# Two arrays woven into one on one Trainium2 core: every 32 KiB row of the loads moved as two pieces of 16 KiB

## Chip, cores and metric

One core of a Trainium2 chip runs the kernel. The metric is the device time of one execution in microseconds (us); smaller is better. The kernel before took 314.11 us, the median of three runs (314.11, 314.11 and 314.13 us).

## What is computed

Two float32 arrays of 32 x 256 x 1024 elements are woven: the even places of the last axis of the result come from x, the odd places from y.

```python
result = np.zeros((batch, seq, dim * 2), dtype=np.float32)
result[..., 0::2] = x
result[..., 1::2] = y
```

Nothing is calculated. Each input is 33.55 MB, the result 67.11 MB, so 67.11 MB are read and 67.11 MB written.

## The kernel before, in words

The flat arrays are cut into n = 8 tiles. A tile of x (or y) is 128 partitions x 8192 float32, that is 128 rows of 32 KiB, 4 MiB in all. A tile of the result is twice that, and is worked in two halves (h = 0 and h = 1) of 4 MiB. On the chip there are two buffers for x tiles (`xt`), two for y tiles (`yt`), used by even and odd tiles, and two for result halves (`ot`), one for each h. DMA means a transfer between the chip's outer memory and these buffers.

Three engines take part, each with its own list in program order:

- **SyncE (SP) issues the loads**, on its own ring of DMA work (q1 in the profile). The first x tile comes as two DMAs of 2 MiB (L42, L43), whose rows are 16 KiB each, since they take half of the columns. Then for each tile k, L50 loads x and L53 loads y, 4 MiB each with rows of 32 KiB. From k = 2 on, L50 waits until the second x copy of tile k - 2 is done (`woven`, L48), and L53 until its second y copy is done (L52), because they overwrite the buffers that these copies read.
- **VectorE (DVE) weaves.** For each tile and half, L67 copies half of the x tile to the even columns of `ot[h]`, and L70 copies half of the y tile to the odd ones. Before L67 of half 0 it waits for the x load (L60); before L67 of either half for the store that last read `ot[h]` (L64); before L70 of half 0 for the y load (L69). Each copy raises `woven` by 1. The order is L67 and L70 of half 0, then L67 and L70 of half 1.
- **ScalarE (ACT) issues the stores**, on another ring (q10). For each tile and half it waits for `woven` (L74) and issues one DMA of 4 MiB with rows of 32 KiB (L83). The very first half is stored in two DMAs: a quarter of the columns (L77, 1 MiB, rows of 8 KiB) and the rest (L81, 3 MiB, rows of 24 KiB).

The two rings are served by the same 16 DMA engines. A DMA of 128 rows gives every engine 8 rows; the trace has one packet record for each row, and one small record of 4 bytes on each engine that signals the end.

In what follows, x3 is the load of tile 3 of x, y3 that of y, and S0_3 and S1_3 are the stores of the two halves of tile 3.

Of the kernel before, what the change touches and what calls it, by code (L numbers as in the profile page):

```python
# [3 lines left out]


def _interleave(nc, x, y, out):
    P = 128
    W = 8192
    H = W // 2  # L10

    total = 1
    for s in x.shape:
        total *= s
    n = total // (P * W)
    assert n * P * W == total

    def rows(ap, names, k):
        flat = ap.rearrange("b s d -> (b s d)")
        return flat[k * names : (k + 1) * names].rearrange("(p w) -> p w", p=P)  # L20

    fp32 = mybir.dt.float32
    xt = [nc.alloc_sbuf_tensor(f"xt{b}", [P, W], fp32).ap() for b in (0, 1)]
    yt = [nc.alloc_sbuf_tensor(f"yt{b}", [P, W], fp32).ap() for b in (0, 1)]
    ot = [nc.alloc_sbuf_tensor(f"ot{b}", [P, W], fp32).ap() for b in (0, 1)]

    xsem = [nc.alloc_semaphore(f"xsem{b}") for b in (0, 1)]
    hsem = nc.alloc_semaphore("hsem")
    qsem = nc.alloc_semaphore("qsem")
    ysem = [nc.alloc_semaphore(f"ysem{b}") for b in (0, 1)]  # L30
    woven = nc.alloc_semaphore("woven")
    osem = [nc.alloc_semaphore(f"osem{b}") for b in (0, 1)]


    cuts = [0, W // 4, W]
    parts = [slice(a, b) for a, b in zip(cuts, cuts[1:])]

    xs = [rows(x, P * W, k) for k in range(n)]
    ys = [rows(y, P * W, k) for k in range(n)]
    os_ = [rows(out, 2 * P * W, k) for k in range(n)]  # L40

    nc.sync.dma_start(out=xt[0][:, :H], in_=xs[0][:, :H]).then_inc(xsem[0], 16)  # L42
    nc.sync.dma_start(out=xt[0][:, H:], in_=xs[0][:, H:]).then_inc(hsem, 16)  # L43

    for k in range(n):
        b = k % 2
        if k >= 2:
            nc.sync.wait_ge(woven, 4 * (k - 2) + 3)  # L48
        if k:
            nc.sync.dma_start(out=xt[b], in_=xs[k]).then_inc(xsem[b], 16)  # L50
        if k >= 2:
            nc.sync.wait_ge(woven, 4 * (k - 2) + 4)  # L52
        nc.sync.dma_start(out=yt[b], in_=ys[k]).then_inc(ysem[b], 16)  # L53

    for k in range(n):
        b = k % 2
        for h in (0, 1):
            c = slice(h * H, (h + 1) * H)
            if h == 0:
                nc.vector.wait_ge(xsem[b], 16 * (k // 2 + 1))  # L60
            elif k == 0:
                nc.vector.wait_ge(hsem, 16)
            if k:
                nc.vector.wait_ge(osem[h], 16 * k)  # L64
            if (k, h) == (1, 0):
                nc.vector.wait_ge(qsem, 16)
            nc.vector.tensor_copy(out=ot[h][:, 0::2], in_=xt[b][:, c]).then_inc(woven, 1)  # L67
            if h == 0:
                nc.vector.wait_ge(ysem[b], 16 * (k // 2 + 1))  # L69
            nc.vector.tensor_copy(out=ot[h][:, 1::2], in_=yt[b][:, c]).then_inc(woven, 1)  # L70

    for k in range(n):
        for h in (0, 1):
            nc.scalar.wait_ge(woven, 4 * k + 2 * h + 2)  # L74
            if (k, h) == (0, 0):
                for c in parts[:-1]:
                    nc.scalar.dma_start(  # L77
                        out=os_[k][:, c], in_=ot[h][:, c]
                    ).then_inc(qsem, 16)
                c = parts[-1]  # L80
                nc.scalar.dma_start(out=os_[k][:, c], in_=ot[h][:, c]).then_inc(osem[h], 16)  # L81
                continue
            nc.scalar.dma_start(  # L83
                out=os_[k][:, h * W : (h + 1) * W], in_=ot[h]
            ).then_inc(osem[h], 16)

    nc.scalar.wait_ge(osem[0], 16 * n)
    used = sorted(s.num for s in [*xsem, hsem, qsem, *ysem, woven, osem[0]])
    assert used == list(range(used[0], used[-1] + 1)), used
    nc.scalar.sem_clear(range(used[0], used[-1] + 1))  # L90
    nc.sync.nop(nofuse=True).wait_op(osem[1], 16 * n, "sem-ge").then_inc(
        osem[1], -16 * n
    )


def kernel(tc, x, y, out):
    nc = tc.nc
    tc.close()
    tc.compile()

    _interleave(nc, x, y, out)

    blocks = nc.main_func.blocks
    for engine in (mybir.EngineType.SP, mybir.EngineType.SP):
        opening = blocks[0].instructions
        at, moved = next(
            (b, i)
            for b in blocks[1:]
            for i in b.instructions
            if i.engine == engine and i.opcode == "DMACopy"  # L110
        )
        assert not (moved.sync_info and moved.sync_info.on_wait)
        body = at.instructions
        body.remove(moved)
        gate = next(
            n
            for n, i in enumerate(opening)
            if i.engine == engine and i.opcode == "Drain"
        )
        opening.insert(gate, moved)  # L120
        at.instructions = body
        blocks[0].instructions = opening


# [1 line left out]
_INS = ['x', 'y']  # L126
_OUTS = [((32, 256, 2048), 'float32')]


# [23 lines left out]
```

## Time and profile before

| What | Value | Where from |
|---|---|---|
| median of three runs | 314.11 us | the times |
| span of the profiled execution, first to last instruction | 312.9 us | the page |
| the profiled execution's own time | 312.9 us of span, and about 1.2 us around it, taken from the median | worked out: 314.11 - 312.9 |
| bytes moved, mean rate | 134.22 MB, 429 GB/s | the page, part 2 |
| DMA packets | 4896, of which 544 end signals | the page, part 2 |
| VectorE busy | 72.0 us, 32 copies, 2.29 us each | the page, parts 1 and 5 |
| store of 4 MiB, issue to landing, median | 34.1 us | the page, part 6 |
| load of x (4 MiB), of y (4 MiB), issue to landing, median | 24.3 us, 41.5 us | the page, part 6 |

How to read it: the span is cut into 40 slices, and a digit tells in tenths how busy an engine (or the mean of the 16 DMA engines) was in a slice. The share of a ring is the time that its packets took, as a share of what 16 engines had in the span. "Issue to landing" runs from the instruction that hands a DMA to its ring until all its bytes have arrived, so it contains the time that the DMA stands behind others in its ring. A wait is put down to what ended it.

### The profile page before, as it was taken

How to read it: one execution, taken by the hardware profiler on the slowest of the kernel's cores; microseconds unless marked ns; L12 is line 12 of the kernel's file. 1: busy time of each engine (PE TensorE's matmuls, PEld its weight loads, DVE VectorE, ACT ScalarE, POOL GpSimd, SP SyncE). 2: the span in 40 equal slices, each digit the busy share in tenths (PEclk: the TensorE clock that was granted, in tenths of full speed). 3: DMA queues.
4: the chain of work that ended last, by engine and by line, in shares of the span. 5: the costliest groups of instructions: out<-in, count | busy, mean ns of one | idle time of the engine just before them, and what ended most of it. 6: DMA issues, size and time to landing. Idle time of an engine off the chain costs nothing.

```text
span 312.9 us, 114 instructions
## 1 busy us (share of the span) xinstructions
DVE 72.0 (23%) x32; POOL 0.2 (0%) x4
## 2 busy tenths in 40 slices
DVE  0216000501305023050220503205032050415410
POOL 0000000000000000000000000000000000000000
DMA  8999999999999999999999999999999999999998
GB/s 337 467 402 436 436 402 419 452 457 415 427 444 411 461 402 469 402 469 402 469 402 465 406 440 432 423 448 402 469 402 469 402 469 402 469 402 448 423 423 381
DMA packets 4896, 134.22 MB, mean 429 GB/s; under 512 B 544, under 2 KB 544, under 8 KB 544
## 3 DMA queue, kind: packets, MB, share of 16 engines
q1 hardware_dynamic: 2448, 67.11, 50.1%
q10 hardware_dynamic: 2448, 67.11, 49.7%
HBM read 67.11 MB, written 67.11 MB: 429 GB/s over the span
## 4 chain that ended last, share of the span: by engine, by line
DMA 82%; DVE 12%; issue 0%
DMA out_dram<-ot 76%; DMA yt<-in_y_dram 6%; DVE ot L70 6%; DVE ot L67 6%
## 5 line engine op out<-in xcount | busy, mean ns | idle before, releaser
L67 DVE COPY ot<-xt 128x4096 f32<-128x4096 f32 x16 | 36.7, 2295 | 213.8 <-DMA out_dram<-ot 206.5
L70 DVE COPY ot<-yt 128x4096 f32<-128x4096 f32 x16 | 36.6, 2288 | 12.3 <-DMA yt<-in_y_dram 12.3
L137 POOL MEMSET const-bfloat16-1.0<- 128x1 bf16 x1 | 0.1, 103 | 0.0
L137 POOL MEMSET const-uint8-127<- 128x1 uint8 x1 | 0.1, 102 | 0.0
L137 POOL MEMSET const-float32-0.0<- 128x1 f32 x1 | 0.1, 100 | 0.2 <-issue 0.2
L137 POOL MEMSET const-float32-1.0<- 128x1 f32 x1 | 0.1, 99 | 0.0
## 6 DMA issues: line engine op xcount, KB each, us to landing
out_dram<-ot ACTq DMA_DIRECT2D x15, 4096.0 KB, 34.1
yt<-in_y_dram SPq DMA_DIRECT2D x8, 4096.0 KB, 41.5
xt<-in_x_dram SPq DMA_DIRECT2D x7, 4096.0 KB, 24.3
xt<-in_x_dram SPq DMA_DIRECT2D x2, 2048.0 KB, 9.5
out_dram<-ot ACTq DMA_DIRECT2D x1, 3072.0 KB, 32.8
out_dram<-ot ACTq DMA_DIRECT2D x1, 1024.0 KB, 16.3
```

Of the source, the lines that this page charges most:

```text
L67: nc.vector.tensor_copy(out=ot[h][:, 0::2], in_=xt[b][:, c]).then_inc(woven, 1)
L70: nc.vector.tensor_copy(out=ot[h][:, 1::2], in_=yt[b][:, c]).then_inc(woven, 1)
L137: nc = _bacc.Bacc("TRN2", target_bir_lowering=False, num_devices=1)
```

## The change

The loads L50 and L53 no longer go through the usual call but through a helper that lays out both sides, the outer memory's and the buffer's, as 128 rows x 2 pieces x 16 KiB before it makes the DMA. The bytes, the buffers, the semaphores, the waits and the order of issue stay as they were. There are 15 such loads (7 of x, 8 of y). The two first loads of x (L42, L43) and all stores are unchanged.

```diff
+QUEUES = {
+    mybir.EngineType.SP: "qSPDynamicHW",
+    mybir.EngineType.Activation: "qActDynamicHW",
+}
+
+
+def _piece_copy(engine, out, in_, s):
+
+    ins, outs = (
+        engine.lower_ap_dma(ap.rearrange("p (s w) -> p s w", s=s)) for ap in (in_, out)
+    )
+    return engine.add_instruction(
+        mybir.InstDMACopy(
+            mode="Copy",
+            name=engine.bass.get_next_instruction_name(),
+            engine=engine.engine,
+            ins=ins,
+            outs=outs,
+            queue=QUEUES[engine.engine],
+        )
+    )
...
         if k:
-            nc.sync.dma_start(out=xt[b], in_=xs[k]).then_inc(xsem[b], 16)
+            _piece_copy(nc.sync, xt[b], xs[k], 2).then_inc(xsem[b], 16)
         if k >= 2:
             nc.sync.wait_ge(woven, 4 * (k - 2) + 4)
-        nc.sync.dma_start(out=yt[b], in_=ys[k]).then_inc(ysem[b], 16)
+        _piece_copy(nc.sync, yt[b], ys[k], 2).then_inc(ysem[b], 16)
```

## The prediction

> **What bounds the kernel now.** The chain of waits is read first, because it names a culprit; its opening and one later round:
>
> ```profile
> 1.90 19.99 DMA yt<-in_y_dram
> 21.89 0.02 issue
> 21.91 2.29 DVE ot L70
> 24.20 2.20 DVE ot L67
> 26.41 2.21 DVE ot L70
> 28.62 0.02 issue
> 28.64 48.16 DMA out_dram<-ot
> ...
> 120.08 34.17 DMA out_dram<-ot
> ```
>
> By this the stores bound the kernel: VectorE waits for a store, weaves for 4.5 us, and the next store takes 34.17 us. The waits say the same (L67 waited 206.5 us for stores, L70 once for a y load, 12.3 us). But 34.17 us for 4 MiB is long, so the second view is whether the DMA engines had anything better to do. The page's slices and rings:
>
> ```profile
> DMA  8999999999999999999999999999999999999998
> q1 hardware_dynamic: 2448, 67.11, 50.1%
> q10 hardware_dynamic: 2448, 67.11, 49.7%
> ```
>
> and busy time by stretches (columns: stretch, its length, VectorE and GpSimd busy, clock, DMA share, GB/s):
>
> ```profile
> 2.00:22.00 20.00, 2.39 (x2) 0.00 (x0) 1.00 1.01 433
> 57.00:250.00 193.00, 44.97 (x20) 0.00 (x0) 1.00 1.00 433
> ```
>
> 50.1% + 49.7% is 99.8% of 16 engines: the 16 DMA engines are never idle, from the first packet (0.99 us after the first issue, by the trace's packet records) to the last (0.38 us before the end of the span). Loads alone (2 to 22 us) run at 433 GB/s, and loads mixed with stores (57 to 250 us) at the same 433. So the bound is the sum of all packets. The chain only tells whose turn it was. The time can change in two ways: packets cost more or fewer ns per byte, or the engines fall idle somewhere.
>
> **How two rings share an engine.** This decides the second way, and the first store shows it. Its two DMAs have rows of 8 and 24 KiB and run beside loads with rows of 32 KiB. The DMA view of 29 to 40 us (8 KiB stores in q10):
>
> ```profile
> q1 hardware_dynamic: 136, 3.93, 85.3%
> q10 hardware_dynamic: 123, 0.92, 19.7%
> ```
>
> and of 42 to 56 us (24 KiB):
>
> ```profile
> q1 hardware_dynamic: 127, 3.64, 60.2%
> q10 hardware_dynamic: 112, 2.75, 45.6%
> ```
>
> The columns are packets, MB, share of time. The packet counts are nearly equal both times (136 to 123, 127 to 112), the bytes 4.3 to 1 and 1.3 to 1. The rings take turns packet by packet, whatever a packet holds. The prices in the packet records are 309, 611, 912 and 1213 ns for 8, 16, 24 and 32 KiB. Turns of 309 + 1213 ns, 8 a DMA, make 12.2 us; the store of 1 MiB landed 16.3 us after issue, of which 4.4 us were before its first packet.
>
> **The change part by part.**
>
> (a) *More packets.* 15 loads x 128 rows become two packets each: 1920 more, 120 for each engine. Upper price: 2 x 611 - 1213 = 9 ns, times 120 = 1.08 us. Lower price, from the end signals in the same records while loads ran alone: one engine's second half of x0 (8 packets of 16 KiB) took 4.862 us from signal to signal, y0 (8 of 32 KiB) 9.681; 2 x 4.862 - 9.681 = 0.043 us, less one signal of 0.009, is 0.034 us for a load of 4 MiB, and 15 loads make 0.51 us. I take 0.6, near the second, since it is time between events and not packets' own durations, which overlap a little (they sum to 311.84 us for each engine in 311.48 us of time). A gain is excluded: a 16 KiB packet costs more than half of a 32 KiB packet in both readings.
>
> (b) *Turns.* A turn of the two rings was 32 KiB against 32 KiB. It becomes 16 KiB of load against 32 KiB of store: while both have work, stores get two thirds. Call U the time of 4 MiB at full rate: two stores and two loads took 38.72 us (stores landed at 115.53 and 154.25), so U = 9.68. A store beside loads took 2 U = 19.4; it now takes 8 turns x (1.209 + 0.607) = 14.5 us, in which the loads advance by half a tile array.
>
> Before, the loads ran ahead: two tiles were loaded or in line when the first store began, and equal turns kept that lead; the stores held the weaving back. Now the lead melts. By hand: the first store packets come at 28 us, with x1 at 0.67. S0_0 takes 8 x (0.307 + 0.607) + 8 x (0.908 + 0.607) = 19.4 us, to 47.4; loads gain 1.0. S1_0 takes 14.5, to 61.9; y1 lands near 57. S0_1 and S1_1 run from about 62.5 to 91.5; x2 lands near 85, and y2 lacks 0.77 at 91.5. The store ring is empty, and y2 has all turns until 99. From tile 2 on, VectorE waits at L70 for y.
>
> Steady state, counted from y_k's last packet: 0.36 us to landing (x0: last signal at 6.97, L67 at 7.33), 0.02, L70 for 2.29, 0.04 until ACT issues S0_k (24.20 to 24.24): 2.71 us. Its first packet comes 0.99 us later on idle rings (L42), 4.4 us later behind queued loads (L77: 24.24 to 28.64). S0_k and S1_k take 2 x 14.5. So S1_k ends 32.7 to 36.1 us after y_k, while y_(k+1) ends after 2 U of loads and 2 U of stores, at 38.7. When y lands, the store ring has been dry for 2.6 to 6 us. In mid-run this costs nothing: x_(k+1) and y_(k+1) stand in the load ring, since their buffers came free when tile k - 1 was woven. The L67 copies, the other L70 and SP's issues (0.33 us) lie beside it.
>
> (c) *The end.* After y7 no load is left to cover that dry spell. Before, y7's last packet passed by 278 us, with 35 us of stores queued behind it. Now nothing moves from y7's last packet until S0_7's first: 2.71 + 0.99 = 3.70 us. The engines then also start cold: the first 16 KiB packets of L42 took 1145 ns and more where 611 is usual, and its 8 packets 0.8 to 1.1 us longer than the next 8. A cold store is not in the trace; 0 to 1.1 us, I take 0.4. S1_7 is woven (4.4 us) under S0_7 (9.7 us).
>
> Sum: 0.6 + 3.7 + 0.4 = **+4.7 us**, with bounds 0.51 + 3.7 + 0 = 4.2 and 1.08 + 3.7 + 1.1 = 5.9. The profiled span of 312.9 becomes 317.6; 1.2 us lie outside it. On the median: 314.11 + 4.7 = **318.8 us**, likeliest range 318.3 to 320.0.
>
> **Rivals.**
>
> *Equal turns stay.* If the two pieces of a row, contiguous on both sides, go in one turn, the loads keep their lead, the end stays covered, and only (a) remains: 314.6 to 315.2. For it: no transfer before has two pieces in a row. Against: each row's packet in the two windows ended the turn. Chance 0.09. The Trainium skill, DMA: Bandwidth & Descriptors, section Queues, rings and completion order, speaks for this rival: an engine is said to drain a whole packet of typically 9 to 17 descriptors from one ring before it switches. By that rule two pieces of a row would share a turn, and the time would be this rival's. The trace disagrees where it can be seen: the counts 136 to 123 are turns of one row each, and an engine's 8 rows of the 1 MiB store, drained at once, would have taken 8 x 0.309 = 2.5 us and not 12.
>
> *Partial cover.* If stores get less than two thirds, S1_6 is still moving when y7 lands and hides part of the 3.7 us. The point is 38.7 us for 2 stores that begin 3.7 to 7.1 us after y: 31.6 to 35 us instead of 29, so a share of 0.55 to 0.61. Time 315.2 to 318.3. Chance 0.08.
>
> *Not slower: the pieces are joined again.* Somewhere between the helper and the engines the two contiguous pieces of a row become one 32 KiB packet. Place: the packets of q1; price 0; it decides if the count stays at 4896. Time 314.1. For it: nothing but contiguity; against: the two-piece layout is made explicitly on both sides. Chance 0.04.
>
> *Faster: the chain is right.* If stores bound the time, two stores in 29 us instead of 38.7 would save up to 9.6 us in each of six or seven rounds, about 60 us, giving 254 us. It decides only if the engines can move more than 433 GB/s; a share of 1.00 and the fixed ns per packet speak against it. Chance 0.02.
>
> *Slower still*, over 320.0: a longer restart, or 69 instead of 45 packets and signals for each engine lined up by the first five loads holding up issues. No row shows a limit there; chance 0.04.
>
> **How the numbers follow.** Forecast 0.73 (318.3 to 320.0), partial cover 0.08, equal turns 0.09, joined 0.04, faster 0.02, slower still 0.04. The range reaches down through partial cover and a little up: 315.2 to 320.3, about 0.82. A change of 0.2% (0.63 us) is about what can be told from none here: same is joined 0.04 and half of equal turns 0.05; faster 0.02; the rest, 0.89, slower.
>
> **What would show it.** (a) 4896 + 1920 = 6816 packets. (b) Beside stores, q1 and q10 with equal packet counts in a stretch, at half the bytes. S0 lands 18 to 20 us after its issue instead of 34.1; the y loads take far longer than 41.5 (about 68: issued 9 us after y_(k-1), landing at 77). VectorE's long wait moves from L67 on stores to L70 on y. (c) A gap of about 4 us in DMA near 294 to 298 us, then two stores of 9.7 us alone. Wrong would be: L67 still waiting 200 us for stores, no gap before the last two stores, or a rate other than 433 GB/s in the middle.

## The result: 3.7% slower

The changed kernel takes 325.98 us (median of 6 runs, 324.18 to 326.77) against 314.14 us before: a ratio of 1.0371, 95% interval 1.0351 to 1.0390. Slower was forecast, but by 4.7 us; it is 11.8, and the time lies outside the range of 315.2 to 320.3. The profiled execution has a span of 324.63 us against 312.86, so 11.77 us are to be found. In the changed kernel L90 and L93 are the copies that were L67 and L70, L18 is the helper's DMA (all split loads), L106 the stores.

The slices, packets and rings from the page after:

```profile
DMA  9999999999999999999999999999999999994599
DMA packets 6816, 134.22 MB, mean 413 GB/s; under 512 B 544, under 2 KB 544, under 8 KB 544
q1 hardware_dynamic: 4368, 67.11, 49.2%
q10 hardware_dynamic: 2448, 67.11, 48.3%
```

There are 1920 packets more, all in the load ring, as forecast. The rings' shares sum to 97.5% instead of 99.8%, and two slices near the end are half empty (4 and 5). The hole lies where the forecast put it, but is larger.

The DMA view of the changed kernel from 108 to 134 us, while both rings have work (packets, MB, share of time):

```profile
q10 hardware_dynamic: 242, 7.41, 66.4%
q1 hardware_dynamic: 243, 3.72, 33.5%
```

One packet each in turn, 243 to 242, so stores get two thirds: the forecast mechanism. Sorted by engine (how is said below), the records of these 26 us change ring every time, the small end signals counted in: 469 pairs of neighbours, and none from the same ring. The Trainium skill, DMA: Bandwidth & Descriptors, section Queues, rings and completion order, would have an engine drain some 9 to 17 descriptors of one ring before it switches; this trace disagrees, with one row's piece to a turn.

The waits of VectorE (us in all, times, longest), before and after, and then issue to landing of the large DMAs after:

```profile
DVE ot L67 <- DMA out_dram<-ot: 206.5, 14, 29.0
DVE ot L70 <- DMA yt<-in_y_dram: 12.3, 1, 12.3
```

```profile
DVE ot L93 <- DMA yt<-in_y_dram: 111.2, 8, 16.3
DVE ot L90 <- DMA out_dram<-ot: 101.0, 7, 20.9
DVE ot L90 <- DMA xt<-in_x_dram: 24.0, 2, 16.7
```

```profile
out_dram<-ot ACTq DMA_DIRECT2D x15, 4096.0 KB, 20.8
yt<-in_y_dram SPq DMA_DIRECT2D x8, 4096.0 KB, 73.0
```

The wait for y went from 12.3 us, once, to 111.2 us, in every tile. A store lands 20.8 us after issue instead of 34.1, and a y load 73.0 instead of 41.5. All this is the forecast's picture, though it put the y loads at about 68. What it lacked shows in the end. The last stretch before the change, and then four stretches after it (stretch, its length, VectorE and GpSimd busy, clock, DMA share, GB/s):

```profile
278.00:312.90 34.90, 8.99 (x4) 0.00 (x0) 1.00 0.97 421
```

```profile
60.00:289.00 229.00, 51.76 (x23) 0.00 (x0) 1.00 1.01 427
289.00:301.20 12.20, 0.00 (x0) 0.00 (x0) 1.00 0.60 254
301.20:304.60 3.40, 3.15 (x2) 0.00 (x0) 1.00 0.00 0
304.60:324.60 20.00, 3.55 (x2) 0.00 (x0) 1.00 0.98 419
```

Before, the engines were busy almost to the end. After, the third line is the pause that was forecast: no DMA for 3.4 us while VectorE weaves. The second line was not forecast. For 12 us ahead of the pause only 0.60 of the 16 engines' time is used, although y7 has not landed: some engines are through with it, others are not. And the first line runs at 427 GB/s instead of 433, more than the new packets cost. The tile's rhythm, by the copies that wait for y (start, length, and in brackets the wait):

```profile
141.46 2.30 DVE L93 COPY ot<-yt 128x4096 f32<-128x4096 f32 x1 [15.80 <-DMA yt<-in_y_dram]
181.56 2.30 DVE L93 COPY ot<-yt 128x4096 f32<-128x4096 f32 x1 [15.68 <-DMA yt<-in_y_dram]
221.52 2.29 DVE L93 COPY ot<-yt 128x4096 f32<-128x4096 f32 x1 [15.59 <-DMA yt<-in_y_dram]
261.36 2.29 DVE L93 COPY ot<-yt 128x4096 f32<-128x4096 f32 x1 [16.27 <-DMA yt<-in_y_dram]
301.45 2.30 DVE L93 COPY ot<-yt 128x4096 f32<-128x4096 f32 x1 [15.80 <-DMA yt<-in_y_dram]
```

A round takes 40.0 us, not 38.7. The packet records tell why. Each load ends with one signal on each of the 16 engines, and it has landed when the last has come. Time between its first and its last signal, in us:

| kernel | y2 | y3 | y4 | y5 | y6 | y7 |
|---|---|---|---|---|---|---|
| before | 0.24 | 0.24 | 0.24 | 0.24 | 0.24 | 0.24 |
| changed | 1.8 | 2.7 | 4.0 | 5.9 | 8.1 | 11.9 |

Before, the 16 engines move as one. After, they drift apart: y7's signals come from 289.25 to 301.13 us, the median at 293.45. And packets **stretch**: from 60 us on no packet before took over 40 ns more than the price of its size; in the changed kernel 157 did, by up to 796 ns, 2.90 us for an engine on average. The fastest engine had done all but the last two stores at 294.1, the slowest at 301.1, and the slowest sets the landing. (The signals of y7 lie further apart than that, because the early engines still had store packets to move after it.)

The records name no engine, but they can be sorted by engine. In both kernels every packet that starts between 60 and 301 us starts 3 or 4 ns before the end of an earlier one, so the records fall into 16 unbroken chains, one for each engine. In the changed kernel this shows three things. No engine was idle from 60 us to its last packet ahead of the pause. The same five chains are the last in y3, y4, y5, y6 and y7; their packets stretched by 5.6 to 7.0 us in all, those of the other eleven by 0.5 to 4.0 us. And the very last chain has 25 stretched packets, 6.97 us in all, which is nearly the whole of its lateness in the next table.

So the 11.77 us, along the slowest engine (before, all but the last two stores were done at 293.11):

| part | us | from |
|---|---|---|
| more packets | 0.78 | 120 for an engine x 6.5 ns, measured in e1 below |
| slowest engine late at y7 | 7.24 | 301.13 - 293.11 - 0.78 |
| pause before S0_7 | 3.49 | 304.62 - 301.13 |
| last two stores, cold start | 0.27 | (324.25 - 304.62) - (312.47 - 293.11) |

### The profile page after: what moved, and what is told of

Same layout as the page of the kernel before. It is cut to its first block, busy times and chain, and to the rows that moved or that the text cites. A ratio compares the mean times of both kernels' runs of the same rounds, so it can differ in the third digit from the quotient of the medians.

```text
span 324.6 us, 114 instructions
## 1 busy us (share of the span) xinstructions
DVE 72.1 (22%) x32; POOL 0.2 (0%) x4
## 4 chain that ended last, share of the span: by engine, by line
DMA 50%; another core or an unknown queue 32%; DVE 12%; issue 0%; ACTq 0%; DVEq 0%
DMA out_dram<-ot 44%; DVE ot L93 6%; DMA yt<-in_y_dram 6%; DVE ot L90 6%; ACTq L100 0%; DVEq L87 0%; DVEq L89 0%
## 5 line engine op out<-in xcount | busy, mean ns | idle before, releaser
L90 DVE COPY ot<-xt 128x4096 f32<-128x4096 f32 x16 | 36.7, 2292 | 125.0 <-DMA out_dram<-ot 101.0
L93 DVE COPY ot<-yt 128x4096 f32<-128x4096 f32 x16 | 36.7, 2291 | 111.2 <-DMA yt<-in_y_dram 111.2
## 6 DMA issues: line engine op xcount, KB each, us to landing
out_dram<-ot ACTq DMA_DIRECT2D x15, 4096.0 KB, 20.8
```

## The experiments

Three questions: is it the turns or the two-piece form; do the pause and the lateness come apart; and what makes packets stretch. In the table, time and ratio are against the kernel before on the same chip, "stretched" counts packets over 40 ns above the price of their size after 60 us and their sum for an engine, "spread" is that of the signals of the last load, all from one profiled run of each. The profiled run was the fastest of four in e4, the slowest in e9 and e12, and among the slower ones in e5.

| run | time us | ratio (95%) | stretched | spread us |
|---|---|---|---|---|
| changed kernel | 325.98 | 1.0371 (1.0351 to 1.0390) | 157, 2.90 us | 11.9 |
| e1 loads and stores split | 315.77 | 1.0050 (1.0033 to 1.0067) | 0 | 0.7 |
| e2 stores split | 315.34 | 1.0042 (1.0026 to 1.0057) | 28, 0.20 us | 2.0 |
| e3 loads as two DMAs | 325.08 | 1.0344 (1.0327 to 1.0360) | 232, 3.84 us | 5.5 |
| e4 last two tiles whole | 322.51 | 1.0253 (1.0216 to 1.0291) | 235, 4.25 us | 6.6 |
| e5 only y3 split | 314.38 | 1.0015 (1.0002 to 1.0028) | 5, 0.06 us | 1.4 |
| e6 weave held twice | 320.44 | 1.0202 (1.0187 to 1.0217) | 97, 3.89 us | 0.6 |
| e7 four pieces | 326.28 | 1.0387 (1.0367 to 1.0406) | 158, 1.93 us | 5.5 |
| e8 short line of loads | 325.49 | 1.0362 (1.0342 to 1.0382) | 156, 2.86 us | 11.2 |
| e9 both ways in turn | 316.80 | 1.0105 (1.0059 to 1.0152) | 117, 1.45 us | 5.0 |
| e10 stores held twice | 314.81 | 1.0018 (1.0009 to 1.0028) | 1, 0.02 us | 1.4 |
| e11 split from tile 5 | 321.18 | 1.0220 (1.0205 to 1.0235) | 43, 0.75 us | 3.1 |
| e12 eight engines moved | 315.25 | 1.0027 (1.0017 to 1.0037) | 34, 0.46 us | 3.6 |

**e1: equal turns again.** Against the changed kernel:

```diff
-            nc.scalar.dma_start(
-                out=os_[k][:, h * W : (h + 1) * W], in_=ot[h]
-            ).then_inc(osem[h], 16)
+            _piece_copy(nc.scalar, os_[k][:, h * W : (h + 1) * W], ot[h], 2).then_inc(osem[h], 16)
```

> Loads and all 4 MiB stores in two pieces of 16 KiB: turns are equal again, 16 against 16. Theory A (unequal turns of 16 against 32 KiB both drain the store ring at the end and put the 16 engines out of step): no gap at the end, the signals of one load stay within about 0.5 us over the engines, and only the packets cost: 240 more for each engine at 4 to 9 ns, so 315.1 to 316.3 us. Theory B (the two-piece form itself, or packets of 16 KiB, puts the engines out of step): spreads of several us on both rings and 318 us or more.

```profile
DMA  8999999999999999999999999999999999999998
DMA packets 8736, 134.22 MB, mean 427 GB/s; under 512 B 544, under 2 KB 544, under 8 KB 544
```

315.77 us, inside the range for theory A, and the page shows no hole, although there are still more packets than in the changed kernel. Theory B falls: neither the two-piece form nor 16 KiB packets put engines out of step. The span grew by 1.56 us for 240 packets an engine, which prices a split at 6.5 ns.

**e2: unequal the other way** (loads as before the change, stores as in e1).

> Only the stores in pieces, loads whole: turns unequal the other way, loads get two thirds. The loads' lead stays, so no gap at the end by either theory. Theory A (unequal turns put the engines out of step): stretched packets and a spread of several us, the slowest engine as late as in the changed kernel without its gap of 3.7 us, 318 to 322 us. If the loss needs a store ring that runs dry and not only unequal turns: 314.6 to 315.3 us and a small spread.

315.34 us. 28 packets stretched, by 291 ns at most, and the spread reached 2.0 us. Theory A as put there, that unequal turns alone cost 4 us and more, failed. The other forecast was nearly met in time, but not in its small spread. The likely reason for the low price is that with loads ahead the slowest engine is covered by queued stores; no run isolates this.

**e3: two plain DMAs for each load.**

```diff
-        _piece_copy(nc.sync, yt[b], ys[k], 2).then_inc(ysem[b], 16)
+        for c in (slice(0, H), slice(H, W)):
+            nc.sync.dma_start(out=yt[b][:, c], in_=ys[k][:, c]).then_inc(ysem[b], 16)
```

(The same for x; the waits at L60 and L69 count 32 for a tile.)

> Each load of 4 MiB as two ordinary DMAs of 2 MiB with rows of 16 KiB (left half, right half of the columns) instead of one DMA of two pieces. Turns are 16 against 32 KiB as in the changed kernel. Theory A (turn lengths): about 326 us, the same drift of the engines and the same dry store ring. Theory B (the order in which the two-piece form deals pieces to engines): the engines stay in step and the time is what the prediction made of the dry store ring, 318 to 320 us.

325.08 us, 0.9 us less than the changed kernel, with the same drift (y7's first half spreads over 12.9 us, its second over 5.5). Pieces in one DMA or two DMAs: what counts is the packet.

**e4: tiles 6 and 7 whole.**

```diff
-        _piece_copy(nc.sync, yt[b], ys[k], 2).then_inc(ysem[b], 16)
+        _piece_copy(nc.sync, yt[b], ys[k], 2 if k < 6 else 1).then_inc(ysem[b], 16)
```

> As the changed kernel, but the four loads of tiles 6 and 7 whole. With equal turns for the last two tiles, two stores take 38.7 us again and S1_6 is still moving when y7 lands, so the pause before the last two stores goes. If the pause is all that matters: 315 to 316 us. If the engines' drift matters as well: the slowest engine keeps what it lost in six tiles, about three quarters of 7.6 us, and the time is 318 to 321 us.

Stretches as above, in e4:

```profile
289.00:300.00 11.00, 4.90 (x3) 0.00 (x0) 1.00 0.98 423
300.00:319.00 19.00, 4.19 (x2) 0.00 (x0) 1.00 0.90 386
```

The pause is gone (share 0.98 where it was 0.60 and 0.00), and the median fell by 3.47 us. That this is so near the pause's 3.49 is partly luck, for the four runs lie between 320.38 and 323.35. But 8 us remain in the median, more than the 318 to 321 us expected. Pause and lateness come apart, and the lateness is the larger part: equal turns at the end do not give it back, and packets went on stretching (116 of them, 2.14 us for an engine, after y5, the last load in pieces, had landed at 221.0 us).

**e5: one unequal load, no dry ring** (x whole, y with `2 if k == 3 else 1`).

> Only y3 in two pieces, all else as before the change: turns are unequal for about 29 us, which costs the loads one U (9.7 us) of their lead of some 12 us, so the store ring never runs dry. Time 314.1 to 314.5 us by both theories. Theory A (unequal turns alone put the engines out of step): stretched packets while y3 moves, and the spread of the load signals grows from 0.24 us to 1 us or more. Theory R (it takes a store ring that runs dry and starts again beside loads): no stretched packets there and a spread that stays at 0.24 us.

While y3 moved, one packet stretched, by 55 ns, and the spread stayed at 0.4 us. Afterwards one packet in each load stretched (by 76 to 322 ns, four times) and the spread crept to 1.4. All five are on one chain, so one engine alone fell behind. One unequal load beside engines that are in step does next to nothing, which speaks against theory A in its plain form; whether unequal turns that last do more, this run does not tell (e9 does). Theory R, the dry ring, stood so far.

**e6: the weave held, so the store ring runs dry.** Against the kernel before:

```diff
+            if (k, h) in ((3, 1), (5, 1)):
+                for _ in range(8):
+                    nc.vector.tensor_copy(out=ot[h][:, 1::2], in_=yt[b][:, c]).then_inc(dsem, 1)
+                    again += 1
+                    nc.vector.wait_ge(dsem, again)
             nc.vector.tensor_copy(out=ot[h][:, 1::2], in_=yt[b][:, c]).then_inc(woven, 1)
```

> The kernel before with equal turns and whole loads, but VectorE repeats the last copy of tiles 3 and 5 eight times, so that the next store comes some 18 us later and the store ring runs dry for about 4 to 8 us, twice, while loads still move. Nothing is left out. Theory R (a dry ring that starts again): packets stretch by hundreds of ns when the stores start again, twice, and the engines' signals are apart by 1 us or more afterwards; the time rises by 0 to 2 us. Theory A (unequal turns): the engines stay in step, spread 0.24 us, 314.1 to 314.4 us.

320.44 us, more than either theory gave. The extra copies also held the next y load, so both rings were dry for 1.5 us (176.9 to 178.4 us); then all 16 engines' first packet took 1.05 to 1.44 us too long, and when loads joined again at 205 to 213 us, some 50 packets stretched by up to 1.1 us. After the second hold the 16 load packets from 258.4 us on stretched again, by 0.27 to 1.47 us. So equal turns do not protect from stretching; but the run changed two things at once.

**e7: four pieces** (`4` in place of `2`).

> Loads in four pieces of 8 KiB: turns of 8 against 32 KiB. The pause before the last two stores stays what it was (3.7 us and the cold start), since the last load is followed by the same weave and issue; the packets cost 3 times as much, 1.5 to 3.2 us. If the drift comes once per restart of the store ring, as in the changed kernel (about 7 us): 326 to 329 us. If it grows with the inequality of the turns: over 330 us. If the pause is larger with smaller pieces, the gap before the last two stores shows it.

326.28 us, hardly over two pieces. The packets cost 360 x 6.5 ns = 2.3 us, and the pause is the same (last load packet at 301.25 us, next store at 304.81). The rest of y7's lateness is 301.25 - 293.11 - 2.3 = 5.8 us: the drift does not grow with the inequality of the turns.

**e8: a shorter line of loads** (SyncE waits for the same array's load of one tile earlier before each load).

> The changed kernel, but SyncE issues each load from tile 2 on only when the load of the same array one tile earlier has landed on all engines, so at most two loads stand in the ring and no engine can be further ahead than that. If being far apart makes packets stretch (the drift feeds itself): spread and stretched time fall and the time falls to 320 to 324 us. If the slow engines lose time whatever the others do: 324 to 328 us, with a smaller spread of the load signals but the same lateness of the last one.

SyncE's own waits in e8:

```profile
SPq L77 <- DMA yt<-in_y_dram: 125.1, 6, 23.2
SPq L72 <- DMA xt<-in_x_dram: 124.8, 6, 29.9
```

The loads were held back, and nothing came of it: 325.49 us, an interval that overlaps with the changed kernel's, as many stretched packets, a spread of 11.2 us. A long line of loads does not feed the drift. But two loads in line still leave room for such a spread, so whether engines that are held closer would stretch fewer packets stays open.

**e9: unequal both ways, no dry ring** (y loads split, x whole, stores of half 1 split).

> All y loads in two pieces and x loads whole, the stores of half 1 in two pieces and those of half 0 whole: most turns are unequal, now one way and now the other, and what the loads lose in one they gain in the other, so they keep their lead and the store ring never runs dry. 960 + 1024 packets more make 0.5 to 1.1 us: Theory R (dry ring and restart): 314.7 to 315.5 us, load signals within 2 us over the engines. Theory A (unequal turns by themselves): drift of several us, 317 us or more.

The profiled run was the slowest of four (319.91 us; the others 316.55 to 316.82). Packets stretched in every round, mostly one to five engines at a time, and the spread grew steadily to 5.0 us with a store ring that was never dry. Theory R as the only cause falls here, though three of the runs are but 1.1 to 1.3 us over its range, and only the slowest has a profile. The several us of drift are what theory A forecast, and the median of 316.80 us is just under its 317: in that run lasting unequal turns put engines out of step without a dry ring.

**e10: a clean restart.** The kernel before with two stores held back, and loads issued on time:

```diff
             nc.vector.tensor_copy(out=ot[h][:, 1::2], in_=yt[b][:, c]).then_inc(woven, 1)
+            if (k, h) in ((3, 1), (5, 1)):
+                nc.vector.wait_ge(woven, 4 * k + 4)
+                for _ in range(8):
+                    nc.vector.tensor_copy(out=ot[h][:, 1::2], in_=ot[h][:, 1::2]).then_inc(dsem, 1)
+                    again += 1
+                    nc.vector.wait_ge(dsem, again)
...
+            if (k, h) in ((3, 1), (5, 1)):
+                nc.scalar.wait_ge(dsem, 8 if k == 3 else 16)
```

> The kernel before, whole rows and equal turns, loads issued as before, but the second store of tiles 3 and 5 is issued some 18 us later (VectorE copies the half's odd columns onto themselves eight times first, nothing is left out), so the store ring alone runs dry for 4 to 8 us while the load ring has work. Theory R: packets stretch when the stores start again, the spread grows from 0.24 us to over 0.6 us, and the time rises by 0.3 to 2.5 us although the engines always have work. If a restart alone does nothing and it needs unequal turns as well: no stretched packets, spread 0.24 us, 314.1 to 314.4 us.

The DMA view of 174 to 180 us in e10 has one ring only:

```profile
q1 hardware_dynamic: 96, 2.62, 101.2%
```

The stores came back beside these loads without one stretched packet; the only one in the run is a last store's at 309 us. Two of theory R's signs did come: the median is 0.57 us up, inside its range, and the signals of y5 and y7 lie 1.5 us apart. Neither comes from engines out of step, as the records show when they are sorted into chains here too. In y5 two engines, and in y7 one, had the load's last row about one store packet (1.2 us) earlier than the others, and at the next signals all 16 were within 0.4 us again; before the last two stores they are done at 292.86 to 293.17 us, as in the kernel before (292.88 to 293.12). The profiled run is longer because of one engine, which at 309 us was idle for 0.30 us and then had the stretched packet (0.35 us). So theory R falls: a ring that runs dry and starts again put no engine out of step here. What delayed that one engine in the last stores, and whether it did so in the other nine runs, stays open.

**e11: split from tile 5 on** (`2 if k >= 5 else 1` for x and y).

> Loads in pieces only from tile 5 on (six loads). y5 uses up the loads' lead of some 12 us, so the store ring runs dry only before y6 and y7. The pause before the last two stores is there in full: 3.5 us. If the drift comes by restarts (one instead of five or six, some 1.2 us each): 318.5 to 320 us. If the engines fall apart at once, however often the ring restarts: 323 us or more. If there is no pause without the long drift before it: 315 us.

```profile
60.00:180.00 120.00, 29.14 (x13) 0.00 (x0) 1.00 1.01 434
180.00:285.00 105.00, 24.78 (x11) 0.00 (x0) 1.00 1.00 428
285.00:296.20 11.20, 0.00 (x0) 0.00 (x0) 1.00 0.74 319
```

The rate falls from 434 to 428 GB/s where the split loads begin. The last load ends at 296.14 us and the next store starts at 299.68: a pause of 3.5 us again. Lateness: 296.14 - 293.11 - 48 x 0.0065 = 2.7 us after three split tiles; 7.2 us after seven (and y0) in the changed kernel. It is about 1 us for each tile, with or without a long run before it. 321.18 us is over the range that one restart was to give, and under the 323 us of engines that fall apart at once.

With four traces the lateness of the last chain can be set against the stretching of its own packets: 7.24 and 6.97 us in the changed kernel, 6.98 (300.87 - 293.11 - 0.78) and 6.80 in e8, 5.65 (299.33 - 293.11 - 88 x 0.0065) and 5.69 in e4, 2.72 and 2.64 here. The lateness is the stretching.

**e12: equal turns, engines moved against each other.** The kernel before with one small load behind y4 that gives 8 engines one more packet:

```diff
         nc.sync.dma_start(out=yt[b], in_=ys[k]).then_inc(ysem[b], 16)
+        if k == 4:
+            nc.sync.dma_start(out=px, in_=xs[0][0:8, 0:2048]).then_inc(psem, 16)
```

> The kernel before, whole rows and equal turns, with one small extra load behind y4: 8 rows of 8 KiB into a buffer that nobody reads, which gives 8 of the 16 engines one packet of about 309 ns more, once, and so moves them against the other 8 from some 160 us on. Theory P (packets stretch when the engines' turns fall against each other in another way than the settled one, whatever makes them do so): stretched packets of 100 ns and more after that point, 0.3 to 3 us, and spreads that change from round to round. Theory A (packets stretch because turns are of unequal length): no stretched packet, the spread goes up once by about 0.3 us and stays, 314.2 to 314.7 us.

The small packets passed at 162.1 us. From 162.2 to 162.5 us 13 packets stretched, from 170.9 to 176.0 another 16, then five in 95 us. The extra packet used up a turn, so 8 engines' loads were a whole turn of the two rings behind the other 8: the signals of every store spread over 2.7 us until the loads ran out, and did not drift. So, in this run, stretching came with engines whose turns fall against each other in another way than the settled one, with equal turns too (theory P). With equal turns they settle into a new order.

## Why the prediction was wrong, point by point

- **The bound** (sum of all packets; the chain names the wrong culprit): right, but not at the fixed price for each packet that it was reckoned with. One of the prediction's own signs of being wrong came: 427 GB/s instead of 433 in the middle, where the new packets alone would leave 431 (e1, 60 to 250 us). The stores became faster, 20.8 us instead of 34.1, and the kernel slower.
- **(a) More packets**: right, 0.78 us where 0.6 was taken and 0.51 to 1.08 bounded. But its price was held to be the price of every packet in the new mixture. Stretched packets were no part of (a), and rows showed them: in the kernel before, load packets took up to 1553 ns from 27 to 42 us, when the first stores, with rows of 8 and 24 KiB, joined.
- **(b) Turns**: right to the packet, 243 to 242. The dry spell when y6 lands is 3.1 us (S1_5's last signal 257.9, y6's 261.0; 2.6 to 6 forecast). S0 lands 18.9 to 19.7 us after issue in the chain from tile 2 on (18 to 20 forecast).
- **(b)'s steady state is the step that failed**: "y_(k+1) ends after 2 U of loads and 2 U of stores, at 38.7". That counts 16 engines as one and every packet at its fixed price; stretching was put at nothing. It holds for the median signal: that of y7 came at 293.45 us, within half a us of 99 us plus five rounds of 38.8. But a load has landed when the slowest engine has its rows, and that one was 7.2 us late, 6.97 us of it in stretched packets of its own. So a round took 40.0 us. The signals of the loads drift apart, while those of the stores, issued only after a full landing, stayed within 4 us. In mid-run the engines that are ahead are never idle; they move loads further on. At the end there are none, and the difference falls due at once: this is the 0.60 ahead of the pause.
- **(c) The end**: right. Pause 3.49 us (3.70 forecast), cold start 0.27 (0.4). In e4, where whole loads cover the end, the pause is gone.
- **Rivals**: equal turns, joined pieces (4896 packets), partial cover and faster are excluded by the packet counts, the pause and the sign. "Slower still" came, at a chance of 0.04, and not for the reasons given: the restart cost 0.27 us, and SyncE's issue, 0.60 us instead of 0.33, held nothing up.

Shown: a loss of this size came wherever small load pieces let the stores overtake the loads, in one DMA or in two (e3, e7, e8), and not with equal turns (e1) or with the loads ahead (e2). It has two parts that come apart (e4), and the larger one is stretched packets that fall on some engines more than on others: in four traces they make up the lateness of the last engine to within 0.3 us. Also shown: one unequal load (e5) or a dry ring alone (e10) is not enough, turns that stay unequal put engines out of step without a dry ring (e9), and engines moved against each other stretch packets with equal turns (e12). That unequal turns keep moving the engines against each other, and so never let them settle, fits e9, e11 and the changed kernel, but is argued, not shown. **Open**: what two packets compete for when they stretch, why it was these five chains, and whether they are the same engines from run to run, since a chain has no name.

No version here beats the kernel before.

## What to carry to other kernels

Where two DMA rings share the engines, the size of a packet is a ring's weight: halving it on one side hands the time to the other, so cut rows only where that ring has lead to spare, and look at what is left to cover the last load's landing. A DMA is as late as its slowest engine: when engines are full, compare the first and the last signal of a transfer, since a spread that grows from round to round is a loss that falls due at the end. A chain that names stores is no reason to favour stores while the engines' share is 1.00.

## What the hardware showed that was not expected

- 16 engines at full load kept within 0.3 us of each other for 250 us, with no packet more than 40 ns over its price; one packet of 8 KiB on 8 of them moved them 2.7 us apart for the next 100 us (e12).
- In the changed kernel the lateness was not shared out: five of the 16 engines lost 5.6 to 7.0 us to stretched packets, and eight lost 1.3 us or less.
- A packet's price is not fixed: 32 KiB packets took up to 1967 ns instead of 1213 while both rings had work (e9), and up to 2678 in e6 when loads and stores started again.
- Two rings that start together from empty cost every engine over 1 us in its first load packet (e6), but a store ring that starts alone on idle engines cost 0.27 us over two stores.
